# One encoder layer on one core: kkq's copies made two and two and two steps sooner, both norms in one step, the forward lanes' inverses sent first

## Chip, cores and metric

The kernel runs on one core of one Trainium2 chip. The metric is the device time of one execution in microseconds (us). The kernel before was run three times; a separate execution was profiled.

## What is computed

One layer of a hybrid encoder on two requests of 256 tokens each (512 tokens together, `D_MODEL` 2048), and a final norm:

```python
def encoder_layer(h, ...):
    xn = rmsnorm(h, norm_mix_w)
    proj = xn @ w_in
    y_na = neighbourhood_attention(na(0), na(1), na(2), na_rpb)      # 8 heads
    y_dn = gated_deltanet_bidir(proj[..., OFF_DN:OFF_Z], ...)        # 8 heads, both directions
    h = h + concatenate([y_na, y_dn]) @ w_out
    hn = rmsnorm(h, norm_ffn_w)
    return h + (silu(hn @ w_gate) * (hn @ w_up)) @ w_down

def chunk_gated_delta_rule(q, k, v, g, beta):                        # chunks of 64 tokens
    a_mat = where(strict, einsum(k_beta, k) * decay, 0)
    t_mat = triangular_solve(eye + a_mat, eye)                       # one inverse per head, chunk
    u = t_mat @ v_beta;  w = t_mat @ (k_beta * exp(g))
    qk = where(tri, einsum(q, k) * decay, 0)
    # then a scan over the 4 chunks, which needs u, w and qk of each
```

A triangular inverse of 64x64 is wanted for each of 2 requests, 8 heads, 4 chunks and 2 directions: 128 of them. The kernel holds one in each of the 128 partitions, a "lane". Lanes 0 to 63 are the forward direction, lanes 64 to 127 the backward one.

## The kernel before

**Stages.** The weights are float32. Each block of them is loaded by SyncE (SP) to `w_raw`, rounded by ScalarE (ACT) to `w_hi` (L134), and the rest is made by VectorE (DVE) as `w_lo` (L135); TensorE (PE) then does three products for each pair of blocks (`mm3`, L149). `half_gemm` (L196) is half of a column tile: 8 blocks, 24 matmuls of 512 columns. `w_raw`, `w_hi` and `w_lo` have three buffers each, so the split of a half tile can run at most when the half tile three before it is done. The stages in order are: keys and queries of the delta net (heads 0 to 7, with their Gram matrices); query, key and value of neighbourhood attention (heads 0 to 7, six half tiles a head, called the attention stage below); value and gate of the delta net with its recurrence; `w_out`; the FFN; the final norm.

**Lanes.** While the attention stage keeps PE busy, the generator `lanes()` (L472) makes the 128 inverses on DVE. It loads the Gram matrices from DRAM to `kkq` in the forward half (four GpSimd (POOL) DMAs of 512 KB, "quarters", L479), copies each quarter to the backward half by ACT (L484), makes the norms of keys and queries by Newton steps (`norms`, L488), multiplies by the decay `E` (L517 to L527), clears `W` by a POOL memset (L547), and solves row by row (`prod`, `W`, L557 to L559: 312 DVE instructions). At the end it scales the inverses back to `kkq` (L567 the forward lanes, two instructions; L569 the backward lanes, two instructions) and sends them to DRAM in eight DMAs of 512 KB each (`s_uq`, L573).

**Steps.** `lanes()` stands in the queue `vector_work`. Every `half_gemm` advances it by one `yield` (L204), so one yield is one half tile in program order. It enters the queue when the last Gram matrices are sent (L386). Before the value tile of head 1 of the delta net, whatever is left of it is written out at once (L842). The instructions of an engine run in the order in which the scheduler places them; a wait of one holds all behind it on that engine. Instructions under `pin` keep their program order among themselves; the weight splits are placed ahead (`AHEAD`).

**After the lanes.** `prepare` (L684) loads the inverses of a pair of heads to `uq` (L694, POOL, after four memsets of `uq`, L677), and `recur` (L713) multiplies with them. PE takes its instructions in order, so a recurrence that waits for `uq` holds the gate tiles behind it. The output of each attention head leaves by POOL too (`na_o` made by ACT, L650; `s_na`, L651); the buffer `s0` of `na_o` is that of `na_s` (L613) of the next head.

Of the kernel before, what the change touches and what calls it, by code (L numbers as in the profile page):

```python
# [13 lines left out]
ALU = mybir.AluOpType  # L14
# [11 lines left out]
C = 64  # L26
# [22 lines left out]
CORE_START = 2  # L49
S_GAP = 3  # L50
R_GAP = 2
LANE_START = 6

EARLY = 3
N_GAP = 2
# [15 lines left out]
def hybrid_encoder(ctx: ExitStack, tc: tile.TileContext, xT, w_in, w_ba, w_out, w_gate,  # L71
                   w_up, w_down, w_group, nw_mix, nw_ffn, nw_fin, na_bias, conv_w, lane_par,
                   dn_nw, y):
    nc = tc.nc
    act = nc.scalar.activation
    tt = nc.vector.tensor_tensor
# [5 lines left out]
    def mm(*a, **k):  # L82
        pin(nc.tensor.matmul(*a, **k))  # L83

    def transpose(*a):
        pin(nc.tensor.transpose(*a))
# [38 lines left out]
    s_uq = dp.tile([H * NB, 2, C, 4, 2, C], F32, name="s_uq")  # L125
# [28 lines left out]
    def newton_rsqrt(out, x, pool):  # L154

        a = pool.tile(list(x.shape), F32, tag="nw", bufs=2, name="nw")
        ai, oi = a.bitcast(I32), out.bitcast(I32)
        ts(ai, x.bitcast(I32), 1, None, ALU.logical_shift_right)
        ts(oi, ai, -1, 0x5f3759df, ALU.mult, ALU.add)
        for _ in range(3):  # L160
            stt(a, out, -0.5, x, ALU.mult, ALU.mult)
            tt(a, a, out, ALU.mult)
            stt(out, a, 1.5, out, ALU.add, ALU.mult)
# [28 lines left out]
    def pause(n):  # L192
        for _ in range(n):
            yield
# [36 lines left out]
    def sm_tile():  # L231
        return psm.tile([P, T], F32, tag="s", name="ps_s")

    kkq = cp.tile([P, C, 2, C], F32, tag="c", name="kkq")
# [121 lines left out]
    def kq_post(h, kq, sqh, sql):  # L356
# [28 lines left out]
        if h == H - 1:  # L385
            vector_work.append(lanes())  # L386
# [11 lines left out]
    def vec(nm, w=C):  # L398
        return ln.tile([P, w], F32, tag=nm, name=nm)
# [72 lines left out]
    def lanes():  # L472
        beta, kd, eg, dg, E = (gt[n] for n in ("beta", "kd", "eg", "dg", "E"))
        qq = vec("qq")

        gram = s_gram.rearrange("k n s w c -> (k n) s (w c)")
        quarters = [slice(q * 16, q * 16 + 16) for q in range(4)]
        for sl in quarters:
            nc.gpsimd.dma_start(kkq[half[0], sl].rearrange("p s w c -> p s (w c)"), gram[:, sl])  # L479
        for d in range(2):  # L480
            nc.gpsimd.dma_start(qq[half[d]], s_qq.rearrange("k h b t -> (k h b) t"))
        yield from pause(LANE_START)
        for sl in quarters:
            pin(nc.scalar.copy(kkq[half[1], sl], kkq[half[0], sl]))  # L484
            yield


        def norms(src, nm):  # L488
            x, s, r = vec(nm + "x"), vec(nm + "s"), vec(nm + "r")
            pin(ts(x, src, EPS, None, ALU.add))  # L490
            newton_rsqrt(r, x, ln)
            tt(s, x, r, ALU.mult)
            return s, r

        dgk = kkq.rearrange("p s w c -> p (s w c)")[:, 0:C * 2 * C:2 * C + 1]
        nk, rk = norms(dgk, "nk")
        yield
        _, rq = norms(qq, "nq")
        yield
        rqd = vec("rqd", 2 * C)  # L500
        for i in range(2):
            ts(rqd[:, i * C:i * C + C], rq, QSCALE, None, ALU.mult)
        egd = vec("egd", 4 * C)
        for i in range(2):
            stt(egd[:, i * C:i * C + C], eg, -1.0, rk, ALU.mult, ALU.mult)
            nc.vector.tensor_copy(egd[:, (2 + i) * C:(3 + i) * C], eg)
        Dm, ndm, rb = vec("Dm"), vec("ndm"), vec("rb")
        tt(rb, rk, beta, ALU.mult)
        tt(Dm, rk, rb, ALU.mult)
        ts(ndm, Dm, -1.0, None, ALU.mult)  # L510
        yield

        LN = {(0, 0): 0, (0, 1): 16, (0, 2): 64 + 16, (0, 3): 64,
              (1, 0): 64 + 48, (1, 1): 64 + 32, (1, 2): 32, (1, 3): 48}
        for q in range(2):
            sl = slice(q * 32, q * 32 + 32)
            tt(kkq[:, sl, 1], kkq[:, sl, 1], E[:, sl], ALU.mult)  # L517
            yield

        h0, h1 = half  # L520
        Et = E[h0].rearrange("p s c -> p c s")
        for q in range(4):
            sl = slice(q * 16, q * 16 + 16)
            n = q * 16 + 16
            tt(kkq[h0, sl, 0, :n], kkq[h0, sl, 0, :n], Et[:, sl, :n], ALU.mult)
            tt(kkq[h1, sl, 0, :n], kkq[h1, sl, 0, :n], E[h1, sl, :n], ALU.mult)
            tt(kkq[:, sl, 0, :n], kkq[:, sl, 0, :n], ndm[:, sl, None].broadcast_to([P, 16, n]),  # L527
               ALU.mult)
            yield
        ps = sm_tile()  # L530
        mm(ps[:, :P], ones, dg, start=True, stop=True)
        nc.scalar.copy(egl, ps[:, :P])
        ps = sm_tile()
        for i, v in enumerate((kd, egd[:, :2 * C], egd[:, 2 * C:], rqd)):
            transpose(ps[:, i * P:i * P + P], v, ident)
        p3 = ps[:, :3 * P].rearrange("p (i l) -> p i l", i=3)
        for (hf, st), l0 in LN.items():
            nc.scalar.copy(tab[half[hf], :, st], p3[half[hf], :, l0:l0 + 16])
        for hf in range(2):
            for pp in range(2):  # L540
                l0 = 3 * P + POS[pp][hf] * 16
                nc.scalar.copy(rqs[half[hf], pp], ps[half[hf], l0:l0 + 16])
        yield

        W = ln.tile([P, C, C], F32, tag="E", name="W")
        Wf = W.rearrange("p s c -> p (s c)")
        nc.gpsimd.memset(W, 0.0)  # L547
        nc.vector.memset(Wf[half[0], 0:C * C:C + 1], 1.0)
        nc.vector.tensor_copy(Wf[half[1], 0:C * C:C + 1], Dm[half[1]])
        work = 0  # L550
        for c in range(1, C):
            for s0 in range(0, c, BLK):
                s1 = min(s0 + BLK, c)
                n, j = s1 - s0, c - s0
                pr = ln.tile([P, BLK * C], F32, tag="prod", bufs=2, name="prod")
                pv = pr[:, :n * j].rearrange("p (s j) -> p s j", j=j)
                tt(pv, W[:, s0:s1, s0:c], kkq[:, c, 0, None, s0:c].broadcast_to([P, n, j]),  # L557
                   ALU.mult)
                nc.vector.tensor_reduce(W[:, s0:s1, c], pv, AX.X, ALU.add)  # L559
                work += 2 * n * j + 200  # L560
            if work > LANE_WORK:
                work = 0
                yield

        for q in range(2):
            sl = slice(q * 32, q * 32 + 32)
            tt(kkq[h0, sl, 0], W[h0, sl], rb[h0, sl, None].broadcast_to([64, 32, C]), ALU.mult)  # L567
            yield
            tt(kkq[h1, sl, 0], W[h1, :, sl].rearrange("p s c -> p c s"),  # L569
               nk[h1, sl, None].broadcast_to([64, 32, C]), ALU.mult)  # L570
            yield
        for (hf, st), l0 in LN.items():
            nc.gpsimd.dma_start(  # L573
                s_uq[:, hf, :, st].rearrange("n s w c -> n s (w c)"),
                kkq[l0:l0 + 16].rearrange("p s w c -> p s (w c)"))

    for h in range(H):
        kq = wk.tile([P, 2, T], F32, tag="kq", bufs=2, name="kq")
# [286 lines left out]
    h1 = [xp.tile([P, 8, T], F32, tag=f"x{2 * i + 1}", name=f"h1_{i}") for i in range(2)]  # L865
# [35 lines left out]
    st = st_cm.__enter__()  # L901
# [17 lines left out]
    for n, i in enumerate(pairs):  # L919
# [14 lines left out]
        w = nwf[:, i:i + 1]  # L934
# [414 lines left out]
```

## Time and profile before

| | us |
|---|---|
| median of 3 runs | 2323.63 (2322.30 to 2323.64) |
| the profiled execution | 2322.96 |
| its span on the core | 2321.2 |
| PE busy | 2265.6 (98%) |
| DVE busy | 1762.3 (76%) |
| ACT busy | 1065.8 (46%) |
| POOL busy | 242.7 (10%) |

Times in views of the trace count from the start of the span. A row of the timeline gives the start, the time, engine, line, operation, output and inputs, and in brackets how long the engine had been idle and what ended that. In a row of windows the first number is the length of the stretch, then the busy time of each engine (with its instructions), the clock granted to PE, the share of the DMA engines that was busy, and GB/s. A row of the chain (the work that ended last, followed back) gives start, time and what. A busy PE isn't a PE at full speed: matmuls are pipelined, and the start of the next tells more than the time of one.

### The profile page before, as it was taken

To read this page: it belongs to the slowest core of one execution; us is meant where nothing else is said; L and a number is where in the kernel's file an instruction comes from. 1 tells how busy PE (TensorE), PEld (TensorE's weight loads), DVE (VectorE), ACT (ScalarE), POOL (GpSimd) and SP (SyncE) were. 2 spreads that over 40 slices of the span, in tenths; PEclk is the share of its full clock that TensorE was granted. 3 is DMA by queue.
4 is the path that set the end of the run, shared out by engine and by line. 5 is a ranking of instruction groups with operands and counts; after the bars stand their busy time and mean duration, and the time that the engine had idled before them with its cause. 6 is when DMAs were issued, how large, how long until landed. Compare 5 with 4: busy or idle time off the path is not lost.

```text
span 2321.2 us, 32510 instructions
## 1 busy us (share of the span) xinstructions
PE 2265.6 (98%) x12318; PEld 1930.8 (83%) x12318; DVE 1762.3 (76%) x2688; ACT 1065.8 (46%) x1640; POOL 242.7 (10%) x342
## 2 busy tenths in 40 slices
PE   9999999994999999999999999999999999999998
PEld 7887888883888888888888888888888878878887
DVE  7744499994455644888888888888888778889876
ACT  6777433231333423644444444444444454444435
POOL 2211000002000010100101010101000011010110
PEclk9999999997999999999999999999999999999999
DMA  5334422325323544677777767776767477667772
GB/s 204 130 123 141 142 96 87 105 87 131 101 82 95 197 155 149 210 205 197 198 211 193 207 188 213 200 207 188 212 191 198 140 221 189 178 186 206 189 198 84
DMA packets 112572, 384.73 MB, mean 166 GB/s; under 512 B 14080, under 2 KB 14416, under 8 KB 112160
## 3 DMA queue, kind: packets, MB, share of 16 engines
q1 hardware_dynamic: 77264, 267.17, 33.2%
q0 software_dynamic: 35152, 115.49, 23.3%
q8 instruction: 97, 1.59, 0.3%
q14 instruction: 59, 0.48, 0.1%
HBM read 347.20 MB, written 35.41 MB: 165 GB/s over the span
## 4 chain that ended last, share of the span: by engine, by line
PE 78%; DVE 12%; ACT 4%; issue 3%; DMA 3%; POOL 0%; SPq 0%; DVEq 0%; ACTq 0%; POOLq 0%
PE ps_g L83 23%; PE ps_a L83 14%; PE ps_c L83 14%; PE ps_d L83 14%; PE ps_b L83 7%; PE ps_s L83 5%; DVE w_lo L135 3%; DVE prod L557 3%; DVE W L559 2%; DVE cacc L346 1%; DMA s_uq<-kkq 1%; ACT w_hi L134 1%; PE ps_o L83 1%; ACT E L467 1%; ACT E L469 1%
## 5 line engine op out<-in xcount | busy, mean ns | idle before, releaser
L83 PE MATMUL ps_g<-xhi,w_hi 128*128 128x512 f32 x896 | 359.9, 402 | 1.4 <-DVE on L437 1.4
L83 PE MATMUL ps_g<-xlo,w_hi 128*128 128x512 f32 x896 | 350.8, 392 | 0.4 <-DVE xlo L250 0.3
L83 PE MATMUL ps_g<-xhi,w_lo 128*128 128x512 f32 x896 | 351.0, 392 | 0.0
L134 ACT ACTIVATE w_hi<-w_first 128x1024 fp32r<-128x1024 f32 (+1 forms) x180 | 185.7, 1032 | 286.9 <-PE ps_c L83 162.4
L135 DVE TENSOR_TENSOR w_lo<-w_raw,w_hi 128x1024 fp32r<-128x1024 f32 x166 | 202.6, 1221 | 133.4 <-ACT w_hi L134 132.7
L134 ACT ACTIVATE w_hi<-w_raw 128x1024 fp32r<-128x1024 f32 x166 | 174.8, 1056 | 252.2 <-PE ps_g L83 213.6
L134 ACT ACTIVATE w_hi<-b 128x1024 fp32r<-128x1024 f32 (+1 forms) x180 | 185.7, 1031 | 226.9 <-issue 120.6
L135 DVE TENSOR_TENSOR w_lo<-w_first,w_hi 128x1024 fp32r<-128x1024 f32 (+1 forms) x180 | 213.6, 1186 | 54.7 <-ACT w_hi L134 46.5
L135 DVE TENSOR_TENSOR w_lo<-b,w_hi 128x1024 fp32r<-128x1024 f32 (+1 forms) x180 | 212.9, 1183 | 3.0 <-ACT w_hi L134 2.8
L83 PEld LDWEIGHTS ps_g<-xhi,w_hi 128*128 128x128 f32 x896 | 169.4, 189 | 38.5 <-issue 4.5
L83 PEld LDWEIGHTS ps_g<-xhi,w_lo 128*128 128x128 f32 x896 | 169.0, 189 | 36.9 <-DVE w_lo L135 0.5
L83 PEld LDWEIGHTS ps_g<-xlo,w_hi 128*128 128x128 f32 x896 | 169.3, 189 | 35.1 <-DVE xlo L250 1.1
L83 PE MATMUL ps_a<-xc,w_hi 128*128 128x512 f32 x704 | 176.9, 393 | 2.2 <-DVE p L972 2.2
L83 PE MATMUL ps_d<-xc,w_hi 128*128 128x512 f32 x704 | 176.3, 392 | 0.0
L83 PE MATMUL ps_c<-xc,w_hi 128*128 128x512 f32 x704 | 176.3, 392 | 0.0
L83 PEld LDWEIGHTS ps_a<-xc,w_hi 128*128 128x128 f32 x704 | 126.9, 189 | 25.7 <-issue 3.0
L83 PEld LDWEIGHTS ps_c<-xc,w_hi 128*128 128x128 f32 x704 | 126.6, 189 | 22.6
L83 PEld LDWEIGHTS ps_d<-xc,w_hi 128*128 128x128 f32 x704 | 126.6, 189 | 22.6
L134 ACT ACTIVATE w_hi<-w_second 128x1024 fp32r<-128x1024 f32 (+1 forms) x60 | 61.9, 1032 | 94.4 <-PE ps_d L83 82.6
L83 PEld LDWEIGHTS ps_a<-xc,w_lo 128*128 128x128 f32 x704 | 96.9, 192 | 7.0
L83 PEld LDWEIGHTS ps_d<-xc,w_lo 128*128 128x128 f32 x704 | 96.0, 190 | 6.9
L83 PEld LDWEIGHTS ps_c<-xc,w_lo 128*128 128x128 f32 x704 | 96.0, 190 | 6.9
(361 smaller groups left out, 4246.4 us busy)
## 6 DMA issues: line engine op xcount, KB each, us to landing
w_raw<-in_w_in_dram SPq DMA_DIRECT2D x110, 512.0 KB, 3.2
b<-in_w_gate_dram SPq DMA_DIRECT2D x66, 512.0 KB, 3.9
b<-in_w_up_dram SPq DMA_DIRECT2D x66, 512.0 KB, 5.3
b<-in_w_group_dram SPq DMA_DIRECT2D x48, 448.0 KB, 4.0
w_raw<-in_w_out_dram SPq DMA_DIRECT2D x32, 512.0 KB, 3.6
w_raw<-in_w_down_dram SPq DMA_DIRECT2D x24, 512.0 KB, 3.4
w_second<-in_w_gate_dram SPq DMA_DIRECT2D x22, 512.0 KB, 7.7
w_first<-in_w_gate_dram SPq DMA_DIRECT2D x22, 512.0 KB, 5.1
```

The source lines that it names most:

```text
L83: pin(nc.tensor.matmul(*a, **k))
L134: act(out=hi, in_=src, func=AF.Copy)
L135: tt(lo, src, r32(hi), ALU.subtract)
L346: stt(a3[:, :, lo:hi], x3[:, :, lo + o:hi + o], cw[:, ct, j:j + 1], a3[:, :, lo:hi], ALU.mult, ALU.add)
L467: pin(act(out=E[half[0], s, s:], in_=G[half[0], s:], func=AF.Exp, bias=NG[half[0], s:s + 1]))
L469: pin(act(out=E[half[1], s, :s + 1], in_=G[half[1], :s + 1], func=AF.Exp, bias=NG[half[1], s:s + 1]))
L557: tt(pv, W[:, s0:s1, s0:c], kkq[:, c, 0, None, s0:c].broadcast_to([P, n, j]), ALU.mult)
L559: nc.vector.tensor_reduce(W[:, s0:s1, c], pv, AX.X, ALU.add)
```

## The change

`LANE_START` goes from 6 to 4. The four copies of quarters share two steps in place of four. The norm of the queries is made in the step of that of the keys. That is five yields fewer ahead of the solve. At the end the two L567 instructions come first, then the four DMAs of the forward lanes, then the two L569 instructions and the four DMAs of the backward lanes.

```diff
-LANE_START = 6
+LANE_START = 4
...
         yield from pause(LANE_START)
-        for sl in quarters:
+        for q, sl in enumerate(quarters):
             pin(nc.scalar.copy(kkq[half[1], sl], kkq[half[0], sl]))
-            yield
+            if q % 2:
+                yield
...
         nk, rk = norms(dgk, "nk")
-        yield
         _, rq = norms(qq, "nq")
         yield
...
-        for q in range(2):
-            sl = slice(q * 32, q * 32 + 32)
-            tt(kkq[h0, sl, 0], W[h0, sl], rb[h0, sl, None].broadcast_to([64, 32, C]), ALU.mult)
-            yield
-            tt(kkq[h1, sl, 0], W[h1, :, sl].rearrange("p s c -> p c s"),
-               nk[h1, sl, None].broadcast_to([64, 32, C]), ALU.mult)
-            yield
-        for (hf, st), l0 in LN.items():
-            nc.gpsimd.dma_start(
-                s_uq[:, hf, :, st].rearrange("n s w c -> n s (w c)"),
-                kkq[l0:l0 + 16].rearrange("p s w c -> p s (w c)"))
+        for d in range(2):
+            for q in range(2):
+                sl = slice(q * 32, q * 32 + 32)
+                if d == 0:
+                    tt(kkq[h0, sl, 0], W[h0, sl], rb[h0, sl, None].broadcast_to([64, 32, C]),
+                       ALU.mult)
+                else:
+                    tt(kkq[h1, sl, 0], W[h1, :, sl].rearrange("p s c -> p c s"),
+                       nk[h1, sl, None].broadcast_to([64, 32, C]), ALU.mult)
+                yield
+            for (hf, st), l0 in LN.items():
+                if l0 // 64 == d:
+                    nc.gpsimd.dma_start(
+                        s_uq[:, hf, :, st].rearrange("n s w c -> n s (w c)"),
+                        kkq[l0:l0 + 16].rearrange("p s w c -> p s (w c)"))
```

No instruction is added or taken away. The lines behind L567 stand two to four higher in the changed kernel (L567 is L569 there, L569 is L572, L573 is L577, L615 is L619, L651 is L655). What moves is the order on each engine, at three places.

**The copies on ACT.** This is ACT's order in the attention stage of head 0, before the change. `w_hi_2159` is a half tile's split, `na_s` are the scores of head 0, and L484 is the copy of a quarter.

```order
L134 ACTIVATE w_hi_2159<-w_raw_2157 128x1024
L134 ACTIVATE w_hi_2189<-w_raw_2187 128x1024
L620 ACTIVATE na_s_2122,sm_2126<-na_s_2122,mx_2124 128x256 x2
L620 ACTIVATE na_s_2132,sm_2136<-na_s_2132,mx_2134 128x256
L624 ACTIVATE na_s_2122<-na_s_2122,sm_2126 128x256
L134 ACTIVATE w_hi_2222<-w_raw_2220 128x1024
L624 ACTIVATE na_s_2122<-na_s_2122,sm_2126 128x256
L620 ACTIVATE na_s_2132,sm_2136<-na_s_2132,mx_2134 128x256
L624 ACTIVATE na_s_2132<-na_s_2132,sm_2136 128x256 x2
L134 ACTIVATE w_hi_2274<-w_raw_2272 128x1024
L134 ACTIVATE w_hi_2316<-w_raw_2314 128x1024
L484 COPY kkq_117<-kkq_117 64x2048
```

And this is the same place after it; `w_hi_2191` is the half tile that was `w_hi_2189`, and `w_hi_2226` that was `w_hi_2222`.

```order
L134 ACTIVATE w_hi_2159<-w_raw_2157 128x1024
L484 COPY kkq_117<-kkq_117 64x2048 x2
L134 ACTIVATE w_hi_2191<-w_raw_2189 128x1024
L484 COPY kkq_117<-kkq_117 64x2048 x2
L624 ACTIVATE na_s_2122,sm_2126<-na_s_2122,mx_2124 128x256 x2
L134 ACTIVATE w_hi_2226<-w_raw_2224 128x1024
```

All four copies now stand ahead of the exponentials of head 0 and of `w_hi_2226`, four half tiles sooner.

**The lanes' start on DVE.** Before, the first norm instruction (`nkx`, which needs all of `kkq`) stood behind the value evacuation of head 1 (`ev_vT_2404`), with one `w_lo` between it and the next large product:

```order
L135 TENSOR_TENSOR w_lo_2507<-w_raw_2504,w_hi_2506 128x1024
L622 RECIPROCAL sm_2385<-sm_2385 128x2
L302 TENSOR_TENSOR ev_vT_2404<-ps_g_2313,rstd_118 128x512
L490 TENSOR_SCALAR nkx_2437<-kkq_117 128x64
L158 TENSOR_SCALAR nw_2441<-nkx_2437 128x64
L158 TENSOR_SCALAR nw_2488<-nqx_2484 128x64
L517 TENSOR_TENSOR kkq_117<-kkq_117,E_582 128x32x64
L135 TENSOR_TENSOR w_lo_2572<-w_raw_2569,w_hi_2571 128x1024
```

After it, `nkx` stands right behind the `w_lo` of the half tile `2226`, ahead of the value evacuation of head 0 (`ev_vT_2154`):

```order
L626 RECIPROCAL sm_2126<-sm_2126 128x2
L135 TENSOR_TENSOR w_lo_2227<-w_raw_2224,w_hi_2226 128x1024
L491 TENSOR_SCALAR nkx_2275<-kkq_117 128x64
L158 TENSOR_SCALAR nw_2279<-nkx_2275 128x64
L517 TENSOR_TENSOR kkq_117<-kkq_117,E_582 128x32x64
L626 RECIPROCAL sm_2136<-sm_2136 128x2
L302 TENSOR_TENSOR ev_vT_2154<-ps_g_2065,rstd_118 128x512
```

Some rows on, the last products of this part (L527) stand ahead of the key evacuation of head 1, where they stood behind it before:

```order
L527 TENSOR_TENSOR kkq_117<-kkq_117,ndm_2356 128x16x48
L161 SCALAR_TENSOR_TENSOR nw_2296<-nqr_2294,nqx_2292 128x64
L527 TENSOR_TENSOR kkq_117<-kkq_117,ndm_2356 128x16x64
L162 TENSOR_TENSOR nw_2296<-nw_2296,nqr_2294 128x64
L302 TENSOR_TENSOR ev_kT_2361<-ps_g_2223,rstd_118 128x512
```

**The lanes' end on DVE and POOL.** Before, DVE ended the lanes behind the evacuation and the convolution (`ev_xi`, `cacc`) of head 0's delta-net value:

```order
L346 SCALAR_TENSOR_TENSOR cacc_4320<-ev_xi_4318,cw_89,cacc_4320 128x2x254
L557 TENSOR_TENSOR prod_4505<-W_2922,kkq_117 128x225
L567 TENSOR_TENSOR kkq_117<-W_2922,rb_2565 64x32x64
L559 TENSOR_REDUCE W_2922<-prod_4505 128x15
L135 TENSOR_TENSOR w_lo_4712<-w_raw_4709,w_hi_4711 128x1024
L567 TENSOR_TENSOR kkq_117<-W_2922,rb_2565 64x32x64
L569 TENSOR_TENSOR kkq_117<-W_2922,nks_2438 64x32x64
```

After it, they end ahead of the key evacuation of attention head 7 (`ev_kT_4175`), one head of attention sooner in this order:

```order
L569 TENSOR_TENSOR kkq_117<-W_2732,rb_2357 64x32x64
L559 TENSOR_REDUCE W_2732<-prod_4505 128x15
L660 SCALAR_TENSOR_TENSOR qT_4062<-ps_g_3983,rstd_118 128x512
L135 TENSOR_TENSOR w_lo_4181<-w_raw_4178,w_hi_4180 128x1024
L569 TENSOR_TENSOR kkq_117<-W_2732,rb_2357 64x32x64
L572 TENSOR_TENSOR kkq_117<-W_2732,nks_2276 64x32x64
L135 TENSOR_TENSOR w_lo_4225<-w_raw_4222,w_hi_4224 128x1024
L302 TENSOR_TENSOR ev_kT_4175<-ps_g_4064,rstd_118 128x512
```

On POOL the output of attention head 6 (`na_o_4155`) now stands behind the first of the eight `s_uq`, and the other seven behind it; before, it stood ahead of all eight:

```order
L655 DMA s_na_100<-na_o_3855 128x512
L577 DMA s_uq_99<-kkq_117 16x64x128
L655 DMA s_na_100<-na_o_4155 128x512
L577 DMA s_uq_99<-kkq_117 16x64x128 x7
L655 DMA s_na_100<-na_o_4602 128x512
```

SP's order is the same, and PE's is but for the transposes of the lanes' small factors (`kd`, `egd`, `rqd`), which come five half tiles sooner.

## Prediction

> **What bounds the kernel now.** I read the page first, by slices of the span.
>
> ```profile
> span 2321.2 us, 32510 instructions
> PE   9999999994999999999999999999999999999998
> PEclk9999999997999999999999999999999999999999
> ```
>
> A slice is 58 us. PE is full in all but one slice, the tenth, 522 to 580 us, and there its clock falls too. So the kernel is bound by PE, and only a stall of PE is worth anything. The second view is what PE waited for around that slice (engine, line, releaser: us in total, times, longest).
>
> ```profile
> PE ps_s L83 <- DMA uq<-s_uq: 21.9, 4, 20.1
> PE ps_s L86 <- ACT dvT L350: 8.2, 1, 8.2
> ```
>
> The third is PE's timeline through these waits, with the granted clock in two windows of it.
>
> ```profile
> 543.41 1.21 PE L86 MATMUL ps_s<-ident,dvT 128*128 128x128 f32 x4 [8.22 <-ACT dvT L350]
> 545.12 0.77 PE L83 MATMUL ps_g<-xhi,w_hi 128*128 128x512 f32 x1
> 549.09 0.40 PE L83 MATMUL ps_g<-xhi,w_hi 128*128 128x512 f32 x1
> 550.92 0.39 PE L83 MATMUL ps_g<-xhi,w_lo 128*128 128x512 f32 x1
> 571.41 0.77 PE L83 MATMUL ps_s<-dvn,uq 128*128 128x128 f32 x2 [20.10 <-DMA uq<-s_uq]
> 579.88 0.40 PE L83 MATMUL ps_g<-xhi,w_hi 128*128 128x512 f32 x1
> 580.34 0.39 PE L83 MATMUL ps_g<-xhi,w_lo 128*128 128x512 f32 x1
> ...
> 540.00:545.00 5.00, 1.59 (x7) 1.47 (x8) 4.29 (x8) 1.81 (x4) 5.00 (x7) 0.50 0.95 120
> 575.00:580.00 5.00, 4.48 (x13) 3.66 (x13) 1.08 (x2) 1.78 (x3) 0.00 (x0) 0.52 0.00 0
> ```
>
> PE stands still from 535.19 (543.41 less 8.22) and is back at speed at 580.57. After each wait it works at half clock: up to 549.09, and from 571.41 to 579.88. The chain of waits and POOL's timeline say who is late.
>
> ```profile
> 532.91 3.73 DVE kkq L569
> 542.25 25.43 DMA s_uq<-kkq
> ...
> 543.57 3.65 POOL L677 MEMSET uq<- 128x1024 f32 x4
> 568.31 4.73 POOL L694 DMA_DIRECT2D uq<-s_uq  x7 [8.89 <-DMA s_uq<-kkq]
> ```
>
> DVE ends the lanes at 536.64. The first wait is for a convolution that is queued on DVE behind L567 and L569. The second is for the inverses: the last is written at 567.68, 31.0 us after L569, and then read back. From nkx on DVE has hardly a gap:
>
> ```profile
> 283.31 0.22 DVE L490 TENSOR_SCALAR nkx<-kkq 128x64 f32<-128x64 f32 x1 [2.32 <-ACT kkq L484]
> 304.27 0.68 DVE L302 TENSOR_TENSOR ev_kT<-ps_g,rstd 128x512 f32<-128x512 f32 x1
> 311.96 0.11 DVE L548 MEMSET W<- 64x64 f32 x1 [2.50 <-POOL W L547]
> ...
> 320.00:536.60 216.60, 215.97 (x383) 1.00 0.28 94
> ```
>
> So the lanes are a DVE queue of 253.3 us (283.31 to 536.64) that starts too late.
>
> **Term 1, what goes if the inverses are in time.** From 535.19 to 580.57, 45.4 us, PE did 18 matmuls from 545.12 on and 12 before 580.57 at, full speed, 0.229 us each (8 of them from 549.09 to 550.92): 6.9 us. The eight transposes took 1.7 us at half clock and the eight small uq matmuls, four pairs of 0.77, 3.1: at full clock 0.9 and 1.5. That is 9.3 us of work, so **36 us** can go: 30.1 of waits and 6 of slow clock. The Trainium skill, "TensorE: Matmul & The Clock Gate", What's actually happening, lets the full clock return after some 3.4 us of sustained work; each return would then cost 1.7 us, an estimate from the page, the term would be 33.5 and the time 2298. The rows have 5.7 and 8.5 us of slow clock, so they stand against it, and the sum keeps 36.
>
> **Term 2, the copies on ACT come before their data.** ACT's timeline, the DMA of the quarters, and the scores of heads 0 and 1 in the chain:
>
> ```profile
> 227.52 1.06 ACT L134 ACTIVATE w_hi<-w_raw 128x1024 fp32r<-128x1024 f32 x1 [0.17 <-PE ps_g L83]
> 232.96 1.06 ACT L134 ACTIVATE w_hi<-w_raw 128x1024 fp32r<-128x1024 f32 x1 [4.38 <-PE ps_g L83]
> 240.45 1.04 ACT L134 ACTIVATE w_hi<-w_raw 128x1024 fp32r<-128x1024 f32 x1
> 251.06 1.06 ACT L134 ACTIVATE w_hi<-w_raw 128x1024 fp32r<-128x1024 f32 x1 [3.20 <-PE ps_g L83]
> 252.14 1.91 ACT L484 COPY kkq<-kkq 64x2048 f32<-64x2048 f32 x1
> ...
> L479 POOL DMA_DIRECT2D kkq<-s_gram x4: 512/529/540, 232.0 to 233.6; - x4
> DMA to landing us min/median/max: 5.2/8.7/13.3
> ...
> 235.87 1.73 PE ps_s L83 x8
> 273.45 1.73 PE ps_s L83 x8
> ```
>
> The quarters land from 237.2 (232.0 and 5.2) to 246.9 (233.6 and 13.3). The first copy now stands right behind the split of 227.52, so ACT waits from 228.6 to 237.2, copies as quarters land, and ends the last copy at 246.9 + 1.9 = 248.8. Queued behind it: the split of 232.96 (now about 242, PE wants it one half tile before 251.06: hidden), the exponentials of head 0 (1.2 us), and the split of 240.45, which now ends at 251.1. PE begins with that one at 251.06, where the buffer of the one before it came free; its w_lo ends 1.2 us later, at 252.3, and PE's third matmul wants it at 251.5. That costs **0.8 us**, and the lead of 9.6 us (240.45 + 1.04 to 251.06) is used up.
>
> DVE then begins nkx at 252.3 in place of 283.31, 31.0 us sooner. But the key evacuation of head 1 now has all of L527 ahead of it: 21.0 us of rows as before (283.31 to 304.27) and three more products, 3.3 us by this group's means (product of kkq and E taken as L527).
>
> ```profile
> L527 DVE TENSOR_TENSOR kkq<-kkq,ndm 128x256 f32<-128x256 f32 (+3 forms) x4 | 3.3, 816 | 0.0
> ```
>
> It ends at 252.3 + 24.3 + 0.7 = 277.3. The scores of head 1 want it at 273.45, by then 274.3: **3 us** of PE. For the rest, DVE's 253.3 us hold 40 splits, and PE's 40 half tiles take 40 x 37.58/6 = 250.5 (273.45 less 235.87 is one head of six half tiles). Both run alike, so the lost lead doesn't come back while the lanes last, and each place where DVE's order is dense can cost PE some tenths. I take **2 us** more. Bounds of the whole: nothing (the first quarters land in time and DVE's slack covers), and 16 (the lead of 9.6 lost once more). Taken: 6, nearest to the rows.
>
> **The lanes' end.** 252.3 + 253.3 less the 2.5 us wait for the W memset, which L527 and the query norm now cover, is 503 at the latest, for the convolution is no longer among the rows. PE, 6 us late, is then still in attention head 7. The last inverse lands by 503 + 31 = 534.
>
> **Term 3, what is late next.** POOL, for the loads of uq stand behind s_na of head 7 and the four memsets. ACT's na_o, the landing of such DMAs, and the s_na before:
>
> ```profile
> 529.70 0.56 ACT L650 COPY na_o<-ps_s 128x512 f32<-128x512 f32 x1
> ...
> s_na<-na_o POOLq DMA_DIRECT2D x1, 256.0 KB, 25.3
> ...
> uq<-s_uq POOLq DMA_DIRECT2D x8, 128.0 KB, 3.1
> ```
>
> 530.3 + 6 = 536.3; 0.6 for s_na and 3.65 for memsets: 540.5; eight issues at 0.68 (7 in 4.73) end at 545.9, landed 549.0, the first head's four by 546.3. PE wants them, from 535.19 + 6 with 0.9 of transposes and 4.1 of matmuls, at 546.2, and the second head's 1 us later. I take **2 us**, between 0 and the 2.8 of these rows. The wait of 8.2 us for the convolution goes: the lanes are off DVE.
>
> **Sum.** 36 - 6 - 2 = 28 us off the profiled execution's 2322.96: 2295.0. The median of the runs stands 0.67 above that execution, so **2296**. Sending the forward lanes first moves no end here: their DMAs land long before POOL comes to uq. Its cost is nil while term 3 holds; if POOL were free earlier, it would be worth the time of one L569 row, 3.7 us.
>
> **Rivals.** (a) *s_na of head 6 is caught among the eight s_uq.* The order puts it between the first and the other seven. Behind all eight it took 25.3 us (above). Its buffer is that of the scores of head 7. Issued near 530.3 - 37.6 + 6 = 499, it would land at 524; DVE wants the buffer at about 506 and would stand 18 us, of which a lead like the 9.6 covers about half: 8 us, 2304. Against: only one s_uq is ahead of it. The Trainium skill, "DMA: Bandwidth & Descriptors", Issuing engines are not separate DMA queues, says that DMAs of all issuers interleave on the same 16 engines; the trace agrees, weight loads beside the s_uq took 15.8 us where they took 3.1 ahead of them:
>
> ```profile
> w_raw<-in_w_in_dram SPq DMA_DIRECT2D x2, 512.0 KB, 15.8
> ...
> w_raw<-in_w_in_dram SPq DMA_DIRECT2D x5, 512.0 KB, 3.1
> ```
>
> The loads are issued a half tile or two ahead of their split, and this is hidden as the 9.6 us lead returns.
>
> (b) *The lead stays lost at more places*: term 2 at its bound, 16 us: 2306.
>
> (c) *Slower: every half tile pays.* Place: the w_lo of each of the 40 half tiles, behind the dense order with no lead. Price: about one w_lo, 1.0 us, each: 40 us, so 2324 - 36 + 40 + 2 = 2330. It decides from 0.85 us a half tile (34 over 40). Against: 253.3 against 250.5 us leaves only some 3 us to pay in all.
>
> (d) *It doesn't do what it says*: the lanes start 31 us sooner, but the DVE queue stretches by as much because PE's results set its pace, and the tail stays: 2324, within 2.
>
> **Chances.** Forecast (gain 20 to 37) 0.63; (a) 0.13, (b) 0.11, (d) 0.05, (c) 0.08. What a measurement of this kernel can tell from no change is about 0.2%, 4.6 us. Faster 0.87, same 0.05, slower 0.08. The range takes in the bound of no cost at all (2323.6 - 36 = 2288, a little under it) and (a) and (b), 2286 to 2310, which leaves out (c), (d) and the worst of (a) with (b).
>
> **What would show it.** Right: ACT idle ahead of the first L484 copy until about 237, nkx at 252, L572 over by 503, no wait of PE over 4 us after 530, and a granted clock of 1.0 there. Wrong: a PE wait for w_lo in each head, a DVE wait for s_na of head 6, or PE still waiting for uq over 5 us.

## The result, and the profile after

| | before | changed |
|---|---|---|
| median of 6 runs each (us) | 2322.70 (2320.13 to 2323.64) | 2302.50 (2298.99 to 2306.43) |
| the profiled execution | 2322.96 | 2306.43 |
| its span | 2321.2 | 2304.6 |

The ratio is 0.9914, with a 95% interval of 0.9901 to 0.9926: the changed kernel is 20 us faster. The forecast was 2296 (28 faster), the range 2286 to 2310. The profiled execution is the slowest of the six; this matters below. In the views here and below, only the rows that a reading rests on are shown; `...` stands between two views, or between two engines of one.

The page of the changed kernel, by slices of its span:

```profile
PE   9999999999999999999999999999999999999998
PEclk9999999999999999999999999999999999999999
```

The hole of the tenth slice is gone. PE's waits from 228 to 600 (releaser: us in total, times, longest) are now these:

```profile
PE ps_g L83 <- DVE w_lo L135: 6.0, 4, 4.3
PE ps_s L83 <- DMA uq<-s_uq: 3.0, 3, 2.0
PE ps_g L83 <- ACT w_hi L134: 0.5, 1, 0.5
PE ps_s L83 <- DVE ev_kT L302: 0.3, 1, 0.3
```

The 30.1 us of before are 3.0, and a wait for `w_lo` has come up. It is the attention stage's. The timeline of ACT, DVE, POOL and PE there, by engine:

```profile
237.79 1.90 ACT L484 COPY kkq<-kkq 64x2048 f32<-64x2048 f32 x1 [8.79 <-DMA kkq<-s_gram]
247.25 1.90 ACT L484 COPY kkq<-kkq 64x2048 f32<-64x2048 f32 x1 [1.61 <-DMA kkq<-s_gram]
...
252.39 0.21 DVE L491 TENSOR_SCALAR nkx<-kkq 128x64 f32<-128x64 f32 x1
270.89 3.51 DVE L491 TENSOR_SCALAR nqx<-qq 128x64 f32<-128x64 f32 x1
275.32 1.22 DVE L135 TENSOR_TENSOR w_lo<-w_raw,w_hi 128x1024 fp32r<-128x1024 f32 x1
280.34 0.68 DVE L302 TENSOR_TENSOR ev_kT<-ps_g,rstd 128x512 f32<-128x512 f32 x1
499.79 3.80 DVE L572 TENSOR_TENSOR kkq<-W,nks 64x2048 f32<-64x2048 f32 x1
...
270.84 3.52 POOL L547 MEMSET W<- 128x4096 f32 x1 [23.44 <-DVE kkq L526]
...
276.60 0.56 PE L83 MATMUL ps_g<-xhi,w_lo 128*128 128x512 f32 x1 [4.29 <-DVE w_lo L135]
277.38 0.63 PE L83 MATMUL ps_g<-xlo,w_hi 128*128 128x512 f32 x1
280.35 0.40 PE L83 MATMUL ps_g<-xhi,w_lo 128*128 128x512 f32 x1
281.08 1.99 PE L83 MATMUL ps_s<-ev_kT,qT 128*128 128x256 f32 x8 [0.33 <-DVE ev_kT L302]
```

The copies and the start of the lanes fall where they were forecast (ACT idle to 237.8, `nkx` at 252.4), and so does their end (503.6, forecast 503). But `nqx`, the first instruction of the queries' norm, takes 3.51 us. It starts 0.05 us after POOL's memset of `W` and both end at 274.4. In the profile of before it took 0.19 us and stood ahead of `nkx`, far from the memset (308.32); with both norms in one step it stands behind `nkx`:

```profile
272.77 0.19 DVE L490 TENSOR_SCALAR nqx<-qq 128x64 f32<-128x64 f32 x1
```

The `w_lo` that PE wants at 272.3 (276.60 less 4.29) is queued behind it. After that wait PE works at half clock for a while (granted clock 0.50 from 277 to 280): a matmul takes 0.63 us from about 277 on, and 0.40 again from 280.35.

The tail, on POOL and on PE, and the loads' landing there:

```profile
542.06 0.57 POOL L655 DMA_DIRECT2D s_na<-na_o  x1 [31.78 <-ACT na_o L654]
542.62 3.65 POOL L681 MEMSET uq<- 128x1024 f32 x4
546.21 5.42 POOL L698 DMA_DIRECT2D uq<-s_uq  x8
...
553.35 0.74 PE L83 MATMUL ps_s<-dvn,uq 128*128 128x128 f32 x2 [2.00 <-DMA uq<-s_uq]
560.25 0.40 PE L83 MATMUL ps_g<-xhi,w_hi 128*128 128x512 f32 x1
...
uq<-s_uq POOLq DMA_DIRECT2D x8, 128.0 KB, 4.9
s_na<-na_o POOLq DMA_DIRECT2D x2, 256.0 KB, 5.9
...
540.00:560.00 20.00, 16.99 (x75) 13.78 (x74) 8.13 (x14) 6.25 (x12) 9.56 (x13) 0.83 0.51 142
```

The waits for `uq` add up to 3.0, and the uq matmuls behind them run at half clock (a pair takes 0.74 us), as does everything up to 560.25.

Where the time went is read by laying the two profiles side by side: PE does the same matmuls in nearly the same order, so the start of one matmul in one profile, less its start in the other, is what was lost or won up to there. Two such pairs, of before and of the changed kernel, are the products with the values of the last attention head and the first four of the recurrence behind the inverses:

```profile
526.90 1.89 PE L83 MATMUL ps_s<-pT,vn 128*128 128x256 f32 x8
581.31 0.71 PE L83 MATMUL ps_o<-n,uq 128*128 128x128 f32 x4
```

```profile
537.92 1.89 PE L83 MATMUL ps_s<-pT,vn 128*128 128x256 f32 x8
561.69 0.71 PE L83 MATMUL ps_o<-n,uq 128*128 128x128 f32 x4
```

At the first the changed kernel is 11.0 us late, at the second 19.6 us early. The table has this difference for all the runs below, at matmuls that start at the given time in the profile of before (positive is later than before; `changed` and `again` are two profiles of the same kernel):

| profile | 230 | 265 | 290 | 500 | 600 | 1800 | end |
|---|---|---|---|---|---|---|---|
| changed | 0.4 | 1.1 | 8.9 | 11.1 | -19.6 | -19.7 | -16.5 |
| again | 0.4 | 2.1 | 9.9 | 12.0 | -19.8 | -21.4 | -22.1 |
| steps_only | 0.6 | 1.5 | 9.3 | 11.4 | -20.4 | -20.4 | -18.0 |
| w_on_act | 0.3 | 2.3 | 6.8 | 8.6 | -21.7 | -21.5 | -20.9 |
| uq_early | 0.0 | 1.3 | 9.1 | 11.3 | -25.6 | -25.6 | -25.8 |
| both | 0.7 | 1.7 | 6.9 | 8.0 | -24.8 | -24.6 | -22.3 |
| qnorm | 0.1 | 1.0 | 5.2 | 7.3 | -28.9 | -30.4 | -29.5 |
| start5 | 0.5 | 0.5 | 19.5 | 19.5 | -13.7 | -13.7 | -14.4 |
| start_only | 0.4 | 0.3 | 0.3 | 4.7 | -14.4 | -16.0 | -16.5 |

So the changed kernel loses 10.7 us in the attention stage (0.4 to 11.1), of which 7.8 lie between 265 and 290; it wins 30.7 at the tail; and in this execution it loses 3.2 in the FFN.

### The profile page after: what moved, and what is told of

Same layout as the page of the kernel before. It is cut to its first block, busy times and chain, and to the rows that moved or that the text cites. A ratio compares the mean times of both kernels' runs of the same rounds, so it can differ in the third digit from the quotient of the medians.

```text
span 2304.6 us, 32507 instructions
## 1 busy us (share of the span) xinstructions
PE 2268.3 (98%) x12318; PEld 1930.8 (84%) x12318; DVE 1766.2 (77%) x2688; ACT 1065.1 (46%) x1640; POOL 242.0 (11%) x342
## 4 chain that ended last, share of the span: by engine, by line
PE 82%; DVE 7%; ACT 4%; DMA 4%; issue 2%; POOL 0%; SPq 0%; DVEq 0%; ACTq 0%; POOLq 0%
PE ps_g L83 26%; PE ps_c L83 14%; PE ps_d L83 14%; PE ps_a L83 14%; PE ps_b L83 7%; PE ps_s L83 6%; DVE w_lo L135 2%; DMA w_raw<-in_w_in_dram 1%; ACT w_hi L134 1%; DVE cacc L346 1%; DMA w_second<-in_w_group_dram 1%; ACT E L467 1%; PE ps_o L83 1%; ACT E L469 1%; PE ps_s L86 1%
## 5 line engine op out<-in xcount | busy, mean ns | idle before, releaser
L83 PEld LDWEIGHTS ps_g<-xlo,w_hi 128*128 128x128 f32 x896 | 169.3, 189 | 36.9 <-DVE xlo L250 2.6
```

## The experiments

**again.** The changed kernel as it is, for a second profile.

> The changed kernel once more, for a second profile. If the 2.8 us that the first profile lost in the FFN (at 1881 and 2066, half clock after waits that the kernel before has too) are scatter of a single execution, they change here while the attention stage's 10.7 and the tail's 6.1 come out again within 1 us; the median is within 2 us of 2302.5. If they belong to the change, they come out again too.

Median 2301.78 us, ratio 0.9908 (0.9893 to 0.9923). From 265 to 290 it lost 7.8 us again, and 11.6 in the whole stage (1.7 before 265, where the first profile had 0.7); at 600 it stands at -19.8, where the first stood at -19.6. From 1800 on it won 0.7 where the first lost 3.2. So the first profile's loss in the FFN is scatter of single executions, and with 3.2 us it is most of what sets the 2306.43 of that execution 3.9 above the median. The clock shows what it is made of. At two places of the FFN the changed kernel's first profile works at half clock behind a wait, and `again` doesn't. One is behind 3.4 us at 1878.47 (granted clock 0.77 from 1880 to 1890) and, in `again`, 2.7 us at 1876.04 (1.00 from 1876 to 1881). The other is behind 2.6 us at 2064.62 and, in `again`, 2.4 us at 2060.14 (one window of each, the first profile's first):

```profile
2065.00:2070.00 5.00, 5.00 (x20) 4.31 (x19) 3.92 (x5) 2.67 (x5) 0.00 (x0) 0.66 0.69 134
...
2060.00:2065.00 5.00, 4.86 (x27) 4.26 (x28) 3.79 (x4) 2.62 (x5) 0.00 (x0) 1.00 0.91 177
```

**w_on_act.** The zeros of `W` are copied by ACT.

```diff
-        nc.gpsimd.memset(W, 0.0)
+        nc.scalar.copy(Wf, zcol.broadcast_to([P, C * C]))
```

`zcol` is a column of zeros that is made once, at the start.

> The changed kernel, with W cleared by a copy of zeros on ACT in place of POOL's memset (L547); nothing else. Theory P (POOL's memset holds DVE): in the trace of the changed kernel nqx took 3.51 us where it took 0.19 before, and it ended with the 3.52 us memset; the lead being gone, that is the 4.29 us wait of PE at 276.60 and the half clock behind it. Then nqx takes 0.2 here, the wait falls to about 1.0 (that w_lo ends near 273.2, PE wants it at 272.15), no clock is lost there, PE leaves the attention stage 5 to 6 us late in place of 10.7, and the time is 2302.5 - 5 = 2297 or a little less. Theory C (copies and a dense order): the wait is the lost lead alone, ACT's clearing (about 3.8 us, two copies of 1.9) is one more thing ahead of the splits; the wait stays near 4 and the time within 2 us of 2302.5.

The timeline of DVE, ACT and PE at the same place (line numbers stand two higher here):

```profile
272.03 0.19 DVE L493 TENSOR_SCALAR nqx<-qq 128x64 f32<-128x64 f32 x1
...
271.89 3.61 ACT L549 COPY W<-zcol 128x4096 f32<-128x4096 f32 x1 [10.36 <-DVE kkq L528]
...
274.42 0.50 PE L83 MATMUL ps_g<-xhi,w_lo 128*128 128x512 f32 x1 [1.00 <-DVE w_lo L137]
278.91 1.99 PE L83 MATMUL ps_s<-ev_kT,qT 128*128 128x256 f32 x8 [1.93 <-DVE ev_kT L304]
```

`nqx` takes 0.19 us and PE's wait falls from 4.29 to 1.00, both as theory P has it. But the next wait, for the key evacuation, grows from 0.33 to 1.93: the evacuation still has all of L527 ahead of it. From 265 to 290 the loss is 4.5 in place of 7.8, 3.3 us less. About half of that is in these two waits (2.93 for 4.62), and the other half is clock: the changed kernel has 3.4 us of half clock behind its wait, and here the granted clock stays at 1.00 from 277 to 283. PE leaves the stage 8.3 us late (0.3 to 8.6) and not 5 to 6. The time doesn't show it: 2302.06 us, ratio 0.9912 (0.9897 to 0.9926). In the profile 1.3 more were lost ahead of 265 than in the changed kernel's first one (the quarters' landing differs from run to run: `again` lost 1.0 more there as well), and at the tail PE waited 3.6 us for `uq` in place of 3.0. That the memset holds `nqx`, and PE through it, is shown. Of the 5 us that theory P put on it, this profile shows 3.3 at that place, and the median shows none.

**uq_early.** The buffers `uq` are opened, and cleared, ahead of the loop over the delta net's values.

```diff
     for h in range(0, H, 2):
+        while vector_work:
+            advance(vector_work)
+        open_recurrence()
         vT = []
```

> The changed kernel, with the buffers uq opened and cleared one tile sooner in program order, so that POOL clears them before s_na of head 7 and not after. Theory T (POOL's queue sets the tail): the loads of uq are issued 3.65 us sooner, PE's three waits for uq (3.0 us) and the half clock from 553 to 560 (3.1 us) both go, together 6: 2296.5. Rival: the loads land late because they share the DMA engines with the weights (5.0 us each here against 3.1 before), a wait of 1 us or more stays and the clock falls all the same: a gain below 2 us, 2301.

POOL's timeline:

```profile
510.49 3.65 POOL L681 MEMSET uq<- 128x1024 f32 x4
540.94 0.57 POOL L655 DMA_DIRECT2D s_na<-na_o  x1 [26.81 <-ACT na_o L654]
541.53 4.74 POOL L698 DMA_DIRECT2D uq<-s_uq  x7
```

The loads go out from 541.5 in place of 546.2, PE has no wait at all between 520 and 600, and what is won at the tail is 36.9 us (11.3 to -25.6) in place of 30.7. Median 2298.17 us, ratio 0.9899 (0.9884 to 0.9914). Theory T holds in the profile (6.2 us); the medians are 4.3 apart, and this profiled execution is the fastest of its four runs.

**both.** The two edits together.

> The two edits of the runs w_on_act and uq_early together. If they are two separate losses, they add up: 2302.5 - 5 - 6 = 2291.5, and PE has no wait over 1.5 us between 240 and 600. Rival: PE comes 5 us sooner to the inverses, which have to be there as much sooner, so that the tail takes back what the attention stage gave: 2296 or above.

Median 2298.33 us, ratio 0.9897 (0.9881 to 0.9914): no faster than `uq_early` alone, so the sum did not come out. The attention stage lost 7.3 in place of 11.3 up to 500. (From 265 to 290 it lost 5.2, where `w_on_act` lost 4.5: behind its wait of 1.92 us for the key evacuation the granted clock is 0.50 from 279 to 281, and behind the 1.93 of `w_on_act` it was 1.00.) But then this stands in PE's timeline:

```profile
537.23 3.22 PE L83 MATMUL ps_s<-pT,vn 128*128 128x256 f32 x8 [2.18 <-ACT pT L647]
```

PE, some 3 us sooner at the last head, waits for `pT` of ACT and falls to half clock (0.50 from 538 to 540); between 500 and the matmuls behind that wait 4 us are lost again. ACT's timeline shows that splits ahead of it had waited for their weights while the inverses were on the DMA engines, one of them for 6.1 us (at 519.15) and a later one for 3.9:

```profile
528.33 1.06 ACT L136 ACTIVATE w_hi<-w_raw 128x1024 fp32r<-128x1024 f32 x1 [3.92 <-DMA w_raw<-in_w_in_dram]
536.61 1.05 ACT L647 COPY pT<-ps_s 128x512 f32<-128x512 f32 x2
```

So the rival was right about the sum, at a place that it had not named: what the stage gave was taken back behind it. That the late weights are the cause was not tried, and it isn't the whole of it: in `qnorm` below, which comes sooner still, a split waits 12.1 us for its weights (at 516.94), and PE has no wait for `pT`.

**steps_only.** The changed kernel with the old end.

```diff
-        for d in range(2):
-            for q in range(2):
+        for q in range(2):
...
-                    tt(kkq[h0, sl, 0], W[h0, sl], rb[h0, sl, None].broadcast_to([64, 32, C]),
-                       ALU.mult)
+            tt(kkq[h0, sl, 0], W[h0, sl], rb[h0, sl, None].broadcast_to([64, 32, C]), ALU.mult)
```

> The changed kernel with the old end: the L567 and L569 instructions in turn, then the eight DMAs in the old sequence. By the prediction the forward lanes' being sent first moves nothing: within 2 us of 2302.5, the same waits for uq (3.0 us). Rival: it is worth up to one row of L569, 3.7 us: 2306.

Median 2303.49 us, ratio 0.9920 (0.9906 to 0.9935); PE waits 3.1 us for `uq`. The order on DVE is the same with and without the new end, since the scheduler places one L572 much sooner in any case (at 325.3 in the changed kernel); what differs is only in which sequence POOL sends the eight DMAs. That part of the change moves nothing that could be measured.

**start_only.** The kernel before with LANE_START 4 alone.

```diff
-LANE_START = 6
+LANE_START = 4
```

> The kernel before with LANE_START 4 and nothing else of the change. nkx stands behind head 1's key evacuation (near 273, 10 us sooner than before), all of L517 to L527 ahead of head 1's value evacuation. If the steps saved are what counts, the lanes end 10 us sooner and the tail is 10 shorter, of which a wait for the value evacuation (PE wants it near 294, it runs near 298) takes 5: 2317, between 2312 and 2321. Rival: LANE_START alone carries the gain: 2305 or below.

Median 2306.05 us, ratio 0.9929 (0.9912 to 0.9945). Beside it the kernel before took 2324.68 and the changed one (`again`) 2301.78, so 18.6 us of 22.9 come from this one number. The expected 2317 was wrong, and so was the rival's share; the rival was the nearer, as the rows show (DVE's timeline, then PE's waits from 228 to 600):

```profile
268.15 0.22 DVE L490 TENSOR_SCALAR nkx<-kkq 128x64 f32<-128x64 f32 x1 [2.19 <-ACT kkq L484]
294.95 0.68 DVE L302 TENSOR_TENSOR ev_vT<-ps_g,rstd 128x512 f32<-128x512 f32 x1
515.39 3.85 DVE L569 TENSOR_TENSOR kkq<-W,nks 64x2048 f32<-64x2048 f32 x1
...
PE ps_s L83 <- DMA uq<-s_uq: 7.2, 4, 5.0
PE ps_s L86 <- ACT dvT L350: 3.6, 1, 3.6
PE ps_s L86 <- DVE ev_vT L302: 2.5, 1, 2.5
```

`nkx` runs 15 us sooner than before and not 10, and the lanes end 17 us sooner (519.2 for 536.6). The attention stage loses 4.3, near the 5 expected. Against this kernel the rest of the change starts the lanes another 16 us sooner and gets 4 us for it: the tail wins 30.7 in place of 19.1 (4.7 to -14.4), and the stage loses 10.7 in place of 4.3. Which of that comes from the copies that share their steps, and which from the two norms in one step, was not tried.

**start5.** The changed kernel with LANE_START 5.

```diff
-LANE_START = 4
+LANE_START = 5
```

> The changed kernel with LANE_START 5. Theory D: the third and fourth copy now stand on ACT behind head 0's pT, nkx runs near 266.6 in place of 252.4, and the whole stretch of L517 to L527 still stands ahead of head 1's key evacuation on DVE, which then runs near 290 where PE wants it at 274: a stall of 15 us or more of the scores of head 1. The time is 2308 or above although the copies come when their data is there. Rival (theory C, the cost is ACT waiting for the copies' data): with the copies later the attention stage loses less than 5 us and the time is 2298 to 2302.

Median 2307.57 us, ratio 0.9931 (0.9917 to 0.9946), 0.4 us under what theory D set as its lower end (2308), and far from the 2298 to 2302 of theory C. PE's timeline at the scores of head 1:

```profile
289.98 3.75 PE L83 MATMUL ps_s<-ev_kT,qT 128*128 128x256 f32 x8 [16.08 <-DVE ev_kT L302]
```

One step later costs 5.8 us (2301.78 for `again` beside it) although ACT waits only 4.1 us for the copies' data (11.5 in the changed kernel) and nothing is lost ahead of 265. `nkx` runs at 262.81, sooner than expected (266.6), and the key evacuation at 289.15, near the 290 expected. So it isn't the step count that sets the stage's loss, and it isn't ACT's wait; it is when the stretch of L517 to L527 on DVE, some 25 us long, begins, and which of PE's evacuations stands behind it. Here and in the changed kernel that is the key evacuation of head 1, which PE wants near 274 (289.98 less 16.08), and here the stretch begins 10.4 us later. In `start_only` it is the value evacuation, which PE wants only at 293.2 (295.78 less 2.55).

**qnorm.** The run `uq_early`, with the queries' norm ahead of the copies and `ndm` in one instruction that needs only `rk` and `rb`.

```diff
         yield from pause(LANE_START)
+        _, rq = norms(qq, "nq")
         for q, sl in enumerate(quarters):
...
         nk, rk = norms(dgk, "nk")
-        _, rq = norms(qq, "nq")
         yield
...
-        ts(ndm, Dm, -1.0, None, ALU.mult)
+        stt(ndm, rk, -1.0, rb, ALU.mult, ALU.mult)
```

> The run uq_early, and beside it the norm of the queries made before the copies (its data lies there since 236, and DVE is idle from 247 to 250), and ndm made from rk and rb by one scalar_tensor_tensor. POOL clears W as in the changed kernel. Theory D (what DVE has queued ahead of head 1's key evacuation is the cost of the early start): that stretch was 27.9 us (252.4 to 280.3); 3.3 of block and some 2.9 of query norm and its table leave it, 21.7 remain, so that the evacuation runs at 274.3, about when PE wants it. No wait over 1.5 us there, PE leaves the attention stage 3 to 5 us late in place of 10.8, and the time is 2298.2 - 6 = 2292. Rival: what is won there is given back where the next dense places come or at the tail: 2297 or above, with waits moved and not gone.

DVE's timeline, and PE's waits from 228 to 600:

```profile
247.50 0.20 DVE L484 TENSOR_SCALAR nqx<-qq 128x64 f32<-128x64 f32 x1 [1.05 <-DMA qq<-s_qq]
271.84 1.22 DVE L135 TENSOR_TENSOR w_lo<-w_raw,w_hi 128x1024 fp32r<-128x1024 f32 x1
273.23 3.03 DVE L527 TENSOR_TENSOR kkq<-kkq,ndm 128x256 f32<-128x256 f32 x4
276.64 0.69 DVE L302 TENSOR_TENSOR ev_kT<-ps_g,rstd 128x512 f32<-128x512 f32 x1
...
PE ps_g L83 <- DVE w_lo L135: 2.8, 4, 0.9
PE ps_s L83 <- DVE ev_kT L302: 1.7, 1, 1.7
PE ps_s L83 <- DMA uq<-s_uq: 0.4, 1, 0.4
PE ps_g L83 <- ACT w_hi L134: 0.3, 1, 0.3
```

Median 2292.88 us (2292.46 to 2296.03), ratio 0.9871 (0.9856 to 0.9886): 32 us under the kernel before in the same runs (2324.68) and the fastest of all; the expectation was 2292. POOL clears `W` as it did, but no tensor_scalar stands beside it. (The queries' data came at 247.5 and not at 236, still in time for that place.) The key evacuation runs 3.7 us sooner than in the changed kernel, 2.3 later than expected, and PE still waits 1.7 us for it, where no wait over 1.5 was expected. The stage loses 7.2 and not the 3 to 5 of the expectation, 4.1 less than `uq_early`. The tail won 36.2. So 4 of the 6 us expected are shown in the stage, and in part they are clock: behind its wait `uq_early` works at half clock (0.50 from 278 to 280), `qnorm` at full clock (1.00 from 275 to 283). For the rest of the agreement with 2292 no row of the stage stands, and it has to be called luck: the last two us are no more than the profiles scatter behind 600, where this one keeps the full clock at the first matmuls of the FFN (1.00 from 968 to 972) and that of `uq_early` doesn't (0.58 from 970 to 974). The norm's place and the shorter way to `ndm` were not tried apart.

## Why the prediction came out as it did

The direction, the mechanism and the range were right; the size was 7 us too large on the median (2302.5 for 2296). No error made good for another: terms 2 and 3 each took 4 to 5 us more than forecast, and term 1 came out as it was put (36.9 for 36). Point by point:

- **Term 1 (36 us).** Right. Where nothing or 0.4 us is left of the wait for `uq`, the tail wins 36.9 (`uq_early`) and 36.2 (`qnorm`).
- **Term 2 (6 us taken, 0 to 16 as bounds).** Too small: 10.7 in the first profile and 11.6 in the second. By its three pieces: the split at 251 was put at 0.8 and cost 0.7 and 1.7; the tenths later on were put at 2 and cost 2.2 and 2.1 (290 to 500); the scores of head 1 were put at 3, and the place where they stand (265 to 290) cost 7.8. **This is the step that failed**: the key evacuation of head 1 was to end at 277.3, a sum of DVE's rows from 283.31 to 304.27 in the profile of before and three products. `nqx` isn't among those rows (it ran at 272.77), and of the memset of `W` the prediction said that L527 and the queries' norm cover the wait for it. They don't cover it; the memset holds the queries' norm itself. In the profile of before DVE stood 2.5 us beside it with nothing to do, here it stands 3.3 us at the place where PE has no lead, and the evacuation ends at 281.0. The wait that this made was another than the one named: 4.29 us for a `w_lo` in the same stretch, and 0.33 for the evacuation. Without the hold (`w_on_act`) the loss there is 3.3 less; that this is as long as the hold is chance, for about half of it is clock. What is left, 4.5 against 3, is the dense order as argued, at full clock: waits of 1.00, 1.93 and, for the next `w_lo`, 0.61, and smaller gaps.
- **Term 3 (2 us taken, 0 to 2.8).** Too small: 36.9 less 30.7 is 6.2. The waits were 3.0; the other 3.2 are half clock behind them, which term 1 counted for the waits of before and term 3 forgot for its own. The loads landed in 4.9 us and not in the 3.1 of the row used, which was one from a quiet stretch. `uq_early` shows cause and price together.
- **The lanes' end and the lead.** The end was right (503.6), and so was that the lead is used up at 251 (PE waits 0.42 us for that `w_lo`). That the lead doesn't come back while the lanes last was not: PE's last wait for a split is at 337.9, and at 500.36 ACT waits 4.4 us for PE to free a buffer, so it is as far ahead there as the buffers let it. The last inverse was to land by 534 and landed near 542.5 (issued at 509.5, 33.0 us to landing). That cost nothing, since POOL came to its loads of `uq` only at 546.2, but "long before" it was not.
- **"Sending the forward lanes first moves no end".** Right by `steps_only`.
- **Rival (a), s_na of head 6 among the eight.** It doesn't occur: `s_na` of head 6 landed 7.4 us after its issue, not 25 (median of the two in the view 5.9). One `s_uq` ahead of it does no harm. **(b)** stands between: 10.7 of 16. **(c)** and **(d)** are excluded by the table: 2 us over the 33 half tiles from 290 to 500, and a tail that went.
- **The granted clock of 1.0 after 530** was named as a sign and didn't come (0.83 from 540 to 560); it belongs to term 3.

By terms the profile of `again` gives 36.9 - 11.6 - 5.1 = 20.2 at 600 (it won 31.8 at the tail, 5.1 less than `uq_early`). This only splits up what the profile shows there; that the medians differ by 20.2 too is no further proof, for the same profile ends 22.1 early.

What stays open: 4.2 us are still lost in `qnorm` at head 1 (1.0 to 5.2, from 265 to 290), of which its two waits there are 2.6, and the cause of `both`'s wait for `pT` was read from rows and not tried.

## What to carry to other kernels

A queue that is nearly full can be started sooner without a price only as far as the engine that it feeds has a lead. Ask at each place which of the other work stands behind the block that moves, and when that is wanted: one step later (`start5`) cost 5.8 us more. A wait that was harmless beside an idle engine isn't covered by putting work beside it, if that work is what the wait would hold. And behind a wait that is left over at a tail, reckon with slow clock as well as with the wait. It can cost the same again, as here, or nothing: in `start5` PE waited 3.3 us for `uq` and had full clock behind it (1.00 from 562 to 568).

## What the runs showed of the hardware

A POOL memset holds some DVE instructions and not others. `nqx`, a tensor_scalar on float32 in SBUF, took 3.51 or 3.52 us beside the memset of `W` in each of the five profiles that have them together, and 0.19 beside ACT's copy of the same size. In `start_only` another pair of tensor_scalars came late in that memset (292.89 to 296.40) and was held up to its end; in the profile of before, without it, the pair took 0.28:

```profile
295.55 0.94 DVE L502 TENSOR_SCALAR rqd<-nqr 128x64 f32<-128x64 f32 x2
```

Instructions with two inputs in SBUF were not held: in `qnorm` a `w_lo` took its 1.22 us and the four products of L527 took 3.03, all but most of the last product beside the memset of `W` (271.79 to 275.31; rows above). In the changed kernel four scalar_tensor_tensor instructions, the last three of them beside the memset of `uq`, took 3.10 us (at 541.86), and four without it 3.09 (at 529.52).

The Trainium skill, "SBUF — State Buffer", SBUF: two separate sides, has this: DVE and GpSimd share a pair of ports under an exclusive lock, for which a DVE instruction in a two-port mode has to wait until the GpSimd instruction has ended, whereas one with two inputs in SBUF meets it only if GpSimd reads SBUF, which a memset doesn't. All the rows here agree, with 3.51 us in place of 0.19 as the price; in which mode `nqx` ran, no row shows.

Of PE's clock: how long a wait was doesn't tell alone whether half clock follows. The wait of 1.93 us in `w_on_act` (278.91) was followed by full clock, that of 1.92 in `both` (278.35) by half. Ahead of the first matmuls of the FFN every profile has a wait of 2.16 us; in the changed kernel's first profile the clock granted behind it was 0.50 (978 to 980), in `again` 1.00. In `start5` a wait of 3.31 us (1884.31) was followed by full clock; from 210 us on, each wait of 3.4 us and more in the ten profiles was followed by half. Where it came, half clock lasted some 3.4 us behind the 4.29 (about 277 to 280.35) and some 7 us in the tail (about 553 to 560.25). The Trainium skill, "TensorE: Matmul & The Clock Gate", What's actually happening, has the clock set by free-running windows of about 3.4 us; these rows fit one and two of them, better than the rows of before led the prediction to think, and windows that run on their own fit equal waits with different clocks behind them.
